# Mixture-of-experts stage of a decoder block: experts of at most 64 tokens computed with whole fp32 products from unsplit weights, in two halves of the output partitions

## The chip, the cores and the metric

The kernel runs on one core of one Trainium2 chip. The metric is the device time of one execution in microseconds (us). Three timed runs of the kernel before gave 1683.66, 1673.73 and 1675.67 us, so the median is 1675.67 us. One further execution was profiled; every row below comes from it.

## What is computed

The program is one decoder block over 512 tokens of width 1024: a Mamba-2 mixer and a pooling mixer, then a mixture of 64 experts of width 256 with one shared expert. Only the expert part matters here. The reference, cut to it:

```python
scores = jax.nn.sigmoid((uf @ w_router).astype(jnp.float32))
...
_, top_e = lax.top_k(masked, TOP_K)              # TOP_K = 8 of 64 experts for each of the 512 tokens
wts = wts / jnp.sum(wts, axis=-1, keepdims=True) * ROUTED_SCALE
...
def expert_block(args):                          # at most 128 tokens of one expert
    toks, ws, e = args
    xb = u_pad[toks]
    hid = jax.nn.silu(xb @ we_gate[e]) * (xb @ we_up[e])
    return (hid @ we_down[e]) * ws[:, None]
```

Everything is fp32. 512 tokens with 8 experts each make 4096 pairs. The reference's routing, evaluated on its own inputs, gives these sizes: 2 experts without a token, 32 with 1 to 64 tokens (the first expert, with 49, among them), 19 with 65 to 128, and 11 with more than 128 (at most 165).

## The kernel before

A product of two fp32 matrices is made of three products of reduced-precision halves (type fp32r). A tensor is split into a high part (a cast on ScalarE, line 44) and a low part (a subtraction on VectorE, line 45), and `mm3` (lines 58 to 62) adds high by high, high by low and low by high.

The function `experts` walks over the 64 experts in an order written out by hand (`manual_schedule`). An expert's weights arrive in three raw tiles of 1 MB, loaded by SyncE (`load`, lines 919, 920 and 926): two for gate and up, which together hold eight slices of the contraction, and one for down. There are eight raw tiles in turn, and `load(e + 2)` stands at the end of expert e. Each raw tile is split into a pair of fp32r tiles before use, which frees the raw tile. Expert e's body has, in order: the gate and up product (`gate_up_mm`, 8 slices of three matmuls of 512 columns), the splits of the next expert's first gate-and-up tile and of its own down tile, SiLU and multiply (`gate_act`, lines 946 and 947), the turning of the next expert's gathered tokens by eight TensorE transposes (`turn`, lines 883 to 889), the split of the next expert's second tile, the down product of the expert before (`down`, 12 matmuls), and the turning of the hidden activations (`down_in`, lines 956 to 958). After the body come the index of expert e + 4 (`slot_rows`, line 860), the scatter-add of the expert before (line 983, GpSimd) and the loads.

The number of an expert's tokens is known only at run time. So every engine holds all variants of a body and branches on a register: `n_e <= P` (line 1113), `n_e > 0` (line 1114). A variant for one block of tokens, one for none, and one for two blocks stand behind one another in each engine's program. The branches are instructions of the engine's sequencer, which runs ahead of the engine. The program is fetched from memory as the engine works through it; the profile shows these transfers as DMA queues of the kind "instruction".

Of the kernel before, what the change touches and what calls it, by code (L numbers as in the profile page):

```python
# [24 lines left out]
D = 1024  # L25
NK = 8
H = 32
G = 8
E = 64
NC = 8  # L30
# [814 lines left out]

def slot_onehot(k, pm, nb, eng):

    oh = k.wp.tile([P, NT, nb, P], BF16, name="oh", bufs=2)
    for t in range(NT):
        eng.tensor_scalar(oh[:, t], k.iota[:, :nb, :], pm[:, t:t + 1], None, op0=ALU.is_equal)  # L850
    return oh
# [24 lines left out]
def turn(k, src, x, full=None):  # L876

    nc = k.nc
    xv = src.rearrange("p (q k) -> p k q", k=NK)
    for hf in range(2):  # L880
        ps = k.xt.tile([P, 512], F32, name="xt", tag="xt")
        for q in range(4):
            nc.tensor.transpose(ps[:, q * P:(q + 1) * P], xv[:, hf * 4 + q, :], k.ident)  # L883
        ks = slice(hf * 4, hf * 4 + 4)
        pv = ps.rearrange("p (q t) -> p q t", q=4)
        if full is not None:
            nc.scalar.copy(full[:, ks, :], pv)
        nc.scalar.copy(x[0][:, ks, :], pv)  # L888
        nc.vector.tensor_sub(x[1][:, ks, :], pv, x[0][:, ks, :].bitcast(F32))  # L889
    return x  # L890


def split_pair(hp, lp):
# [48 lines left out]

def gate_act(k, ps):
# [70 lines left out]
def experts(k, shared):  # L1014
# [71 lines left out]
    gu[0][0].split(k, k.gu0w[0])  # L1086
    gu[0][1].split(k, k.gu1w)
    shared()
    onehot(4)
    load(1)  # L1090
    dn[0].split(k, k.dnw[0])
    turn(k, xg[0], k.xT[0])
    with tc.manual_schedule():
        fetch_over(0)
        fetch_over(1)
        for e in range(E):
            more = e + 1 < E
            xT, xnext = k.xT[e % 2], k.xT[(e + 1) % 2]
            hx, hlast = k.hx[e % 2], k.hx[(e + 1) % 2]
            fetch(e + 2)  # L1100

            def last_down(n):
                if e > 0:
                    down(k, hlast, dn[e - 1], n, k.yl[(e + 1) % 2], idx[e - 1][1][:, 0:1])

            def splits():
                if more:
                    gu[e + 1][0].split(k, k.gu0w[(e + 1) % 2])
                if e > 0:
                    dn[e].split(k, k.dnw[e % 2])  # L1110

            n_e = count(e, (ET.PE, ET.Activation, ET.DVE))
            with tc.If(n_e <= P) as big:
                with tc.If(n_e > 0) as some:
                    g0 = gate_up_mm(k, xT, gu[e])
                    splits()
                    hid = gate_act(k, g0)
                    if more:
                        turn(k, xg[e + 1], xnext)
                        gu[e + 1][1].split(k, k.gu1w)  # L1120
                    last_down(0)
                    last_down(1)
                    down_in(k, hid, hx)
                with some.Else():
                    splits()
                    if more:
                        turn(k, xg[e + 1], xnext)
                        gu[e + 1][1].split(k, k.gu1w)
                    last_down(0)
                    last_down(1)  # L1130
            with big.Else():
                turn(k, k.xg[3 + e % 2], xnext)
                g0 = gate_up_mm(k, xT, gu[e])
                splits()
# [4 lines left out]
                if more:  # L1139
                    turn(k, xg[e + 1], xnext)  # L1140
                last_down(0)
                down_in(k, hid1, k.hx[2])
                last_down(1)
                if more:
                    gu[e + 1][1].split(k, k.gu1w)
                for n in range(2):
                    down(k, k.hx[2], dn[e], n, k.xg[2], idx[e][1][:, 1:2])
            fetch_over(e + 2)
            onehot(e + 5)
# [6 lines left out]
        for n in range(2):  # L1156
            down(k, k.hx[e % 2], dn[e], n, k.yl[e % 2], idx[e][1][:, 0:1])
# [80 lines left out]
def block_kernel(ctx, tc, a, out):  # L1238
# [54 lines left out]
    with ExitStack() as p2:  # L1293
        raw2 = p2.enter_context(tc.tile_pool(name="raw2", bufs=2))
        k.wp = p2.enter_context(tc.tile_pool(name="wp", bufs=1))
        k.raws += [raw2.tile([P, 2048], F32, name="raw", tag="raw") for _ in range(2)]
        k.yl = [k.zp.tile([P, D], F32, name="yl", tag="zs") for _ in range(2)]
        k.hx = [tuple(k.wp.tile([P, 2, P], F32R, name=f"h{n}{i}") for n in "hl") for i in range(3)]
        spx = ExitStack()
        sp = spx.enter_context(tc.tile_pool(name="sp", bufs=1))  # L1300
# [45 lines left out]
```

## Time and profile before

| | |
|---|---|
| timed runs | 1673.73, 1675.67, 1683.66 us |
| profiled execution, whole | 1690.4 us |
| its span, first to last instruction | 1688.7 us |
| mean granted TensorE clock | 0.959 of full speed |
| bytes moved by DMA | 340.26 MB, mean 201 GB/s |

The page gives for each engine its busy time and its number of instructions. PE is TensorE's matmuls, PEld its weight loads, DVE is VectorE, ACT is ScalarE, POOL is GpSimd. An engine name with a "q" behind it is that engine's sequencer. In a timeline, the bracket at the end of a row is the idle time of the engine ahead of it and what ended it; "issue" there means that nothing the profile shows was waited for. A granted clock of 1.00 is 2.4 GHz and 0.50 is 1.2 GHz.

### The profile page before, as it was taken

The page shows a single profiled execution, that of the slowest core. Times are in us where ns is not written, and L with a number is a line of the kernel's source. Part 1 is how long each engine was busy: PE and PEld are TensorE (multiplying, and loading weights), DVE is VectorE, ACT ScalarE, POOL GpSimd, SP SyncE. Part 2 cuts the span into 40 slices and gives each one's busy share as a digit, 9 for nine tenths or more (in the row PEclk, how much of TensorE's full clock was granted, in tenths as well). Part 3 has the DMA queues.
Part 4 walks back from the last instruction along what each step waited for, and adds up shares of the span by engine and source line. Part 5 has one row for each costly group of instructions (what it writes and reads, how often), then busy time and mean ns, then how long its engine had stood idle before and what let it go on. Part 6 is the DMA issues. An engine that isn't in the chain of part 4 may idle for free.

```text
span 1688.7 us, 23424 instructions
## 1 busy us (share of the span) xinstructions
PE 1527.1 (90%) x7900; PEld 1267.4 (75%) x7900; DVE 1280.2 (76%) x1938; ACT 919.2 (54%) x1122; POOL 440.5 (26%) x312
## 2 busy tenths in 40 slices
PE   5999999999999999999898988898899988989980
PEld 5888788787888778887687776787677876777760
DVE  6888878778787974558666769776669889985856
ACT  3555545345343223335565657676567777775752
POOL 5211101002010110320233334332324233441426
PEclk7999999999999999999899999999999999999995
DMA  9442433333342345235967759868879988996954
GB/s 289 116 125 84 142 100 111 101 97 109 95 131 88 107 134 197 88 130 208 356 186 273 245 158 347 308 216 254 278 240 312 350 287 292 314 313 232 326 168 153
DMA packets 152118, 340.26 MB, mean 201 GB/s; under 512 B 15816, under 2 KB 94832, under 8 KB 142272
## 3 DMA queue, kind: packets, MB, share of 16 engines
q1 hardware_dynamic: 135888, 294.94, 51.8%
q0 software_dynamic: 15408, 40.23, 9.3%
q8 instruction: 120, 1.97, 0.5%
q10 hardware_dynamic: 576, 2.10, 0.3%
q14 instruction: 126, 1.03, 0.2%
HBM read 314.00 MB, written 31.01 MB: 204 GB/s over the span
## 4 chain that ended last, share of the span: by engine, by line
PE 53%; DMA 21%; issue 10%; DVE 9%; POOL 3%; ACT 3%; POOLq 0%; another core or an unknown queue 0%; SPq 0%; DVEq 0%; ACTq 0%
PE mm L62 8%; PE mm L60 8%; PE mm L61 8%; DMA xg<-u2d,idx 8%; DMA raw<-in_we_up_dram 5%; PE gu L60 4%; PE gu L62 4%; PE gu L61 4%; DMA Y<-xg,idx 4%; DVE wl L45 2%; DMA Y<-yl,idx 2%; PE xt L883 2%; PE sd L476 1%; PE yo L60 1%; PE yo L62 1%
## 5 line engine op out<-in xcount | busy, mean ns | idle before, releaser
L45 DVE TENSOR_TENSOR wl<-raw,wh 128x2048 fp32r<-128x2048 f32 x180 | 422.0, 2358 | 96.8 <-ACT wh L44 86.2
L44 ACT CAST wh<-raw 128x2048 fp32r<-128x2048 f32 x180 | 341.2, 1918 | 88.2 <-PE mm L61 64.2
L983 POOL DMA_INDIRECT Y<-yl,idx x64 | 132.5, 2070 | 482.6 <-ACT hh L957 238.5
L60 PE MATMUL gu<-wh,xh 128*128 128x512 f32 x444 | 184.0, 414 | 8.6 <-issue 6.6
L62 PE MATMUL gu<-wh,xl 128*128 128x512 f32 x444 | 180.3, 406 | 2.1 <-issue 2.1
L61 PE MATMUL gu<-wl,xh 128*128 128x512 f32 x444 | 180.5, 407 | 0.4 <-DVE hl L958 0.4
L60 PE MATMUL mm<-uh,wh 128*128 128x512 f32 x432 | 171.2, 396 | 1.9 <-ACT zs L284 1.9
L62 PE MATMUL mm<-uh,wl 128*128 128x512 f32 x432 | 169.8, 393 | 0.0
L61 PE MATMUL mm<-ul,wh 128*128 128x512 f32 x432 | 169.0, 391 | 0.0
L45 DVE TENSOR_TENSOR pair<-raw,pair 128x2048 fp32r<-128x2048 f32 x66 | 148.5, 2289 | 25.2 <-ACT pair L44 18.4
L871 POOL DMA_INDIRECT xg<-u2d,idx x75 | 126.0, 1680 | 97.6 <-DVE oh L850 27.5
L946 ACT ACTIVATE hid<-gu 128x256 f32<-128x256 f32 x73 | 28.1, 385 | 203.6 <-PE gu L62 203.6
L44 ACT CAST pair<-raw 128x2048 fp32r<-128x2048 f32 x66 | 123.2, 1923 | 15.8 <-DMA raw<-in_ws_up_dram 12.4
L883 PE MATMUL xt<-ident,xg 128*128 128x128 f32 x632 | 89.8, 286 | 36.7 <-issue 20.3
L883 PEld LDWEIGHTS xt<-ident,xg 128*128 128x128 f32 x632 | 84.0, 194 | 43.6 <-issue 36.2
L889 DVE TENSOR_TENSOR xl<-xt,xh 128x512 fp32r<-128x512 f32 x150 | 96.9, 685 | 20.3 <-ACT xh L888 18.8
L60 PEld LDWEIGHTS gu<-wh,xh 128*128 128x128 f32 x444 | 87.9, 198 | 27.5 <-issue 8.1
L888 ACT CAST xh<-xt 128x512 fp32r<-128x512 f32 x150 | 81.5, 590 | 45.2 <-PE xt L883 42.1
L61 PEld LDWEIGHTS gu<-wl,xh 128*128 128x128 f32 x444 | 87.6, 197 | 23.6 <-issue 3.9
L62 PEld LDWEIGHTS gu<-wh,xl 128*128 128x128 f32 x444 | 87.2, 196 | 20.5
L60 PEld LDWEIGHTS mm<-uh,wh 128*128 128x128 f32 x432 | 81.2, 188 | 20.2 <-ACT zs L284 2.3
L947 DVE TENSOR_TENSOR hid<-hid,gu 128x256 f32<-128x256 f32 x73 | 30.4, 417 | 85.7 <-ACT hid L946 85.7
(341 smaller groups left out, 3568.7 us busy)
## 6 DMA issues: line engine op xcount, KB each, us to landing
raw<-in_we_gate_dram SPq DMA_DIRECT2D x124, 512.0 KB
raw<-in_we_up_dram SPq DMA_DIRECT2D x124, 512.0 KB
raw<-in_we_down_dram SPq DMA_DIRECT2D x62, 1024.0 KB
raw<-in_w_in_dram SPq DMA_DIRECT2D x27, 1024.0 KB
raw<-in_w_ada_dram SPq DMA_DIRECT2D x16, 1024.0 KB
big<-in_w_ada_dram SPq DMA_DIRECT2D x16, 512.0 KB
raw<-in_w_in_dram SPq DMA_DIRECT2D x16, 512.0 KB
raw<-in_w_br_ssd_dram SPq DMA_DIRECT2D x8, 1024.0 KB
```

The lines of the kernel that those rows point to most:

```text
L44: nc.scalar.copy(h, raw)
L45: nc.vector.tensor_sub(l, raw, h.bitcast(F32))
L60: nc.tensor.matmul(out, sh, mh, start=first, stop=False)
L61: nc.tensor.matmul(out, sh, ml, start=False, stop=False)
L62: nc.tensor.matmul(out, sl, mh, start=False, stop=last)
L871: k.nc.gpsimd.indirect_dma_start(out=xg[:n], out_offset=None, in_=k.u2d, bounds_check=T - 1, oob_is_err=False, in_offset=bass.IndirectOffs ...
L883: nc.tensor.transpose(ps[:, q * P:(q + 1) * P], xv[:, hf * 4 + q, :], k.ident)
L888: nc.scalar.copy(x[0][:, ks, :], pv)
L889: nc.vector.tensor_sub(x[1][:, ks, :], pv, x[0][:, ks, :].bitcast(F32))
L946: nc.scalar.activation(hid, ps[:, :256], AF.Silu)
L947: nc.vector.tensor_mul(hid, hid, ps[:, 256:])
L983: k.nc.gpsimd.indirect_dma_start(out=k.Y[acc], out_offset=bass.IndirectOffsetOnAxis(ap=idx[0][:n, b:b + 1], axis=0), in_=y[:n], in_offset= ...
```

## The change

An expert with at most 64 tokens takes a variant of its own ("light"). Its weights are not split. `turn_light` turns 64 tokens in one PSUM tile and one copy, without a low part. `gate_up_light` multiplies in plain fp32 straight from the raw tiles: the tokens are the stationary operand (64 columns), gate fills partitions 0 to 63 of the output and up partitions 64 to 127, 16 matmuls of 256 columns. `act_light` turns both and applies SiLU and the product on the turned side. `down_light` does the same with the two halves of the 1024 output columns, 4 matmuls of 512 columns. Experts above 64 tokens are computed as before; the first expert always is. The branch for "no token" is gone: such an expert takes the light variant on what the tiles hold, its loads left out as before.

Because the variant of expert e needs the tokens of e + 1 turned, and the down product of e - 1 done, either of which may be light or not, each variant holds both forms of both steps behind branches of their own. The one-hot of the index moves from the body's end (for e + 5) to its start (for e + 4), in one buffer in place of two.

```diff
-    oh = k.wp.tile([P, NT, nb, P], BF16, name="oh", bufs=2)
+    oh = k.wp.tile([P, NT, nb, P], BF16, name="oh")
...
+def turn_light(k, src, x):
+
+    nc = k.nc
+    xv = src.rearrange("p (q k) -> p k q", k=NK)
+    ps = k.xt.tile([P, 512], F32, name="xt", tag="xt")
+    for kk in range(NK):
+        nc.tensor.transpose(ps[:, kk * LIGHT:(kk + 1) * LIGHT], xv[:LIGHT, kk, :], k.ident[:LIGHT, :LIGHT])
+    nc.scalar.copy(x, ps.rearrange("p (k t) -> p k t", k=NK))
...
+def gate_up_light(k, x, units):
+
+    nc = k.nc
+    ps = k.gu.tile([P, 512], F32, name="gu", tag="gu")
+    for kk in range(NK):
+        w = units[kk // 4].raw.rearrange("p (s k f) -> p s k f", k=4, s=2)
+        for s in range(2):
+            nc.tensor.matmul(ps[s * LIGHT:(s + 1) * LIGHT, :256], x[:, kk, :], w[:, s, kk % 4, :], start=kk == 0, stop=kk == NK - 1)
+    return ps
+
+
+def evict_light(k, ps):
+    hid = k.wp.tile([P, 256], F32, name="hid", bufs=2)
+    k.nc.scalar.copy(hid, ps[:, :256])
+    return hid
+
+
+def act_light(k, hid, x):
+
+    nc = k.nc
+    hv = hid.rearrange("p (q j) -> p j q", j=2)
+    ps = k.ht.tile([P, 2, P], F32, name="ht", tag="ht")
+    for j in range(2):
+        nc.tensor.transpose(ps[:, j, :], hv[:, j, :], k.ident)
+    nc.scalar.activation(x, ps[:, :, :LIGHT], AF.Silu)
+    nc.vector.tensor_mul(x, x, ps[:, :, LIGHT:])
+
+
+def down_light(k, x, unit, y, w):
+
+    nc = k.nc
+    ps = k.yo.tile([P, 512], F32, name="yo", tag="yo")
+    for j in range(2):
+        for n in range(2):
+            nc.tensor.matmul(ps[n * LIGHT:(n + 1) * LIGHT, :], x[:, j, :], unit.raw[:, j * D + n * 512:j * D + n * 512 + 512],
+                             start=j == 0, stop=j == 1)
+    for n in range(2):
+        nc.scalar.activation(y[:LIGHT, n * 512:(n + 1) * 512], ps[n * LIGHT:(n + 1) * LIGHT, :], AF.Copy, scale=w[:LIGHT])
...
+    def by_count(e, engines, light, heavy):
+
+        if e == 0:
+            heavy()
+        elif e < E:
+            with tc.If(count(e, engines) <= LIGHT) as small:
+                light()
+            with small.Else():
+                heavy()
...
+            def light():
+                g = gate_up_light(k, k.xf, gu[e])
+                early_split(e + 1)
+                hid = evict_light(k, g)
+                turned(e + 1)
+                downs(e - 1)
+                act_light(k, hid, k.hT)
+
+            def one():
+                g = gate_up_mm(k, xT, gu[e])
+                early_split(e + 1)
+                split_down(e)
+                hid = gate_act(k, g)
+                turned(e + 1)
+                downs(e - 1)
+                down_in(k, hid, hx)
...
+            def heavy():
+                with tc.If(count(e, every) <= P) as single:
+                    one()
+                with single.Else():
+                    two()
+
+            by_count(e, every, light, heavy)
```

`early_split`, `turned`, `downs` and `split_down` wrap the steps named above; `early_split`, `turned` and `downs` each branch on the count of the expert that they serve. `two` is the body for two blocks, with the same wrapped steps in it.

TensorE's program before, at the place where the variant for one block ends and the variant for an empty expert begins (`ht` is the turned hidden tile, `xt` the turned tokens, `yo` the down product):

```order
L62 MATMUL yo<-pair,hl_6171 128x512
L956 MATMUL ht<-ident,hid 128x128 x2
L1114 UNCONDITIONAL_BRANCH
L883 MATMUL xt<-ident,xg_5332 128x128 x8
L60 MATMUL yo<-pair,hh_6170 128x512
```

From the branch to the start of the next expert stand the variant for none and the variant for two blocks, which an expert of one block jumps over.

TensorE's program now, the start of one expert (`gu<-raw,xf` is the light gate and up product, `yo<-raw,hT` the light down product; lines from 883 on stand one or more further down than before):

```order
L1150 COMPARE_AND_BRANCH
L1164 UNCONDITIONAL_BRANCH
L961 MATMUL gu<-raw,xf 64x256 x16
L1150 COMPARE_AND_BRANCH
L900 MATMUL xt<-ident,xg_5332 128x64 x8
L1150 UNCONDITIONAL_BRANCH
L884 MATMUL xt<-ident,xg_5332 128x128 x8
L1150 UNCONDITIONAL_BRANCH
L1150 COMPARE_AND_BRANCH
L988 MATMUL yo<-raw,hT 64x512 x4
L1150 UNCONDITIONAL_BRANCH
L61 MATMUL yo<-pair,hh_6172 128x512
```

The light variant now stands first, with both forms of the two wrapped steps in it; the variants for one block and for two blocks follow, each with both forms as well. A light expert jumps from its end over all of these; a heavy one jumps over the light variant first.

ScalarE's program before, one expert of one block (`wh` and `pair` are high parts of weights):

```order
L1113 COMPARE_AND_BRANCH
L1114 COMPARE_AND_BRANCH
L44 CAST wh<-raw 128x2048 x2
L946 ACTIVATE hid<-gu 128x256
L888 CAST xh_6486<-xt 128x512 x2
L44 CAST wh<-raw 128x2048
L979 ACTIVATE yl<-yo,wt 128x512 x2
L957 CAST hh_6172<-ht 128x256
L1114 UNCONDITIONAL_BRANCH
```

ScalarE's program now, the start of a light expert:

```order
L1150 COMPARE_AND_BRANCH
L1164 COMPARE_AND_BRANCH
L45 CAST wh<-raw 128x2048
L1164 UNCONDITIONAL_BRANCH x2
L967 COPY hid<-gu 128x256
L1150 COMPARE_AND_BRANCH
L901 COPY xf<-xt 128x512
L1150 UNCONDITIONAL_BRANCH
L889 CAST xh_6488<-xt 128x512 x2
L45 CAST wh<-raw 128x2048
L1150 UNCONDITIONAL_BRANCH
```

The casts of the next expert's weights now stand behind a branch on that expert's count, and its own down tile is not cast at all.

## Rows read from the trace of the kernel before

**Rows 1.** Busy us (instructions) by stretch: expert stage, single blocks.

```profile
core 0: us, PE busy (x) PEld busy (x) DVE busy (x) ACT busy (x) POOL busy (x), PEclk, DMA share, GB/s
797.00:1645.00 848.00, 762.68 (x3944) 628.46 (x3942) 646.03 (x935) 565.70 (x643) 287.61 (x150) 0.95 0.82 272
1278.00:1303.00 25.00, 24.50 (x141) 20.36 (x141) 24.61 (x34) 20.96 (x25) 8.40 (x4) 1.00 1.03 329
```

**Rows 2.** The page's DMA issues: down weights, and results of second blocks.

```profile
raw<-in_we_down_dram SPq DMA_DIRECT2D x62, 1024.0 KB
...
Y<-xg,idx POOLq DMA_INDIRECT x11, 6.3
```

**Rows 3.** Line 946, the SiLU of every block: ns min/median/max, first, last start.

```profile
L946 ACT ACTIVATE hid<-gu x73: 372/385/389, 814.6 to 1636.3; 128x256 f32<-128x256 f32 x73
```

**Rows 4.** ScalarE's timeline (start us, us), SiLU alone: three single blocks.

```profile
1298.57 0.39 ACT L946 ACTIVATE hid<-gu 128x256 f32<-128x256 f32 x1 [1.34 <-PE gu L62]
...
1313.00 0.38 ACT L946 ACTIVATE hid<-gu 128x256 f32<-128x256 f32 x1 [6.07 <-PE gu L62]
...
1322.69 0.39 ACT L946 ACTIVATE hid<-gu 128x256 f32<-128x256 f32 x1 [1.33 <-PE gu L62]
```

**Rows 5.** The same: an expert of two blocks, and the next expert.

```profile
1111.81 0.39 ACT L946 ACTIVATE hid<-gu 128x256 f32<-128x256 f32 x1 [1.30 <-PE gu L62]
...
1130.11 0.39 ACT L946 ACTIVATE hid<-gu 128x256 f32<-128x256 f32 x1 [1.36 <-PE gu L62]
```

**Rows 6.** TensorE's timeline at 1304 us, inside the gap of rows 4.

```profile
1303.93 0.40 PE L60 MATMUL gu<-pair,xh 128*128 128x512 f32 x1
1304.17 0.39 PE L61 MATMUL gu<-pair,xh 128*128 128x512 f32 x1
1307.60 0.79 PE L62 MATMUL gu<-pair,xl 128*128 128x512 f32 x1 [3.04 <-issue]
1308.19 0.63 PE L60 MATMUL gu<-pair,xh 128*128 128x512 f32 x1
```

**Rows 7.** What TensorE waited for, 797 to 1650 us: total, times, longest.

```profile
PE xt L883 <- issue: 20.3, 4, 6.0
PE gu L60 <- issue: 10.5, 4, 3.7
...
PE gu L62 <- issue: 8.3, 3, 3.2
PE ixp L860 <- issue: 7.8, 6, 3.1
...
PE gu L61 <- issue: 4.1, 2, 3.6
```

**Rows 8.** Branches on the count, by sequencer: times, ns shortest/median/longest.

```profile
L1113 PEldq COMPARE_BRANCH  x64: 64/75/5589, 808.0 to 1628.2; - x64
L1113 ACTq COMPARE_BRANCH  x64: 34/34/50, 810.8 to 1630.9; - x64
...
L1114 PEldq COMPARE_BRANCH  x106: 67/188/6792, 808.1 to 1637.2; - x106
```

**Rows 9.** The page's DMA queues, one of program code: packets, MB, share.

```profile
q8 instruction: 120, 1.97, 0.5%
```

**Rows 10.** The same queue in the expert stage, 797 to 1650 us.

```profile
q8 instruction: 89, 1.46, 0.7%
```

**Rows 11.** The same queue, 1416 to 1434 us, the weight queue full.

```profile
q8 instruction: 4, 0.07, 1.5%
```

**Rows 12.** The same queue, 1487 to 1491.5 us, the weight queue running empty.

```profile
q8 instruction: 2, 0.03, 2.7%
```

**Rows 13.** Groups: a weight tile's split, and a plain fp32 product.

```profile
L45 DVE TENSOR_TENSOR wl<-raw,wh 128x2048 fp32r<-128x2048 f32 x180 | 422.0, 2358 | 96.8 <-ACT wh L44 86.2
L44 ACT CAST wh<-raw 128x2048 fp32r<-128x2048 f32 x180 | 341.2, 1918 | 88.2 <-PE mm L61 64.2
...
L458 PE MATMUL sd<-xdec,Bt 128*128 128x256 f32 x48 | 14.7, 388 | 0.0
```

More of the change, by code (lines that the diff above doesn't have):

```diff
@@ L27 @@
 H = 32
+LIGHT = 64
 G = 8
@@ L1092, in experts, with early_split, late_split, turned @@
     turn(k, xg[0], k.xT[0])
+    every, both = (ET.PE, ET.Activation, ET.DVE), (ET.Activation, ET.DVE)
+    def by_count(e, engines, light, heavy):
[6 more added lines that the diff above has]
+                heavy()
+    def early_split(e):
+        if e < E:
+            for engines in (every, both):
+                count(e, engines)
+        def heavy():
+            gu[e][0].split(k, k.gu0w[e % 2])
+        if e < E:
+            with tc.If(count(e, both) > LIGHT):
+                heavy()
+    def late_split(e):
+        gu[e][1].split(k, k.gu1w)
+    def turned(e, split_too=True):
+        def heavy():
+            turn(k, xg[e], k.xT[e % 2])
+            if split_too:
+                late_split(e)
+        by_count(e, every, lambda: turn_light(k, xg[e], k.xf), heavy)
+    def downs(e, parts=(0, 1)):
+        if e < 0:
+            return
+        y, w = k.yl[e % 2], idx[e][1][:, 0:1]
+        def light():
+            if 0 in parts:
+                down_light(k, k.hT, dn[e], y, w)
+        def heavy():
+            for n in parts:
+                down(k, k.hx[e % 2], dn[e], n, y, w)
+        by_count(e, every, light, heavy)
+    def split_down(e):
+        if e > 0:
+            dn[e].split(k, k.dnw[e % 2])
     with tc.manual_schedule():
@@ L1096, in experts, with light, two @@
         for e in range(E):
-            more = e + 1 < E
             xT, xnext = k.xT[e % 2], k.xT[(e + 1) % 2]
-            hx, hlast = k.hx[e % 2], k.hx[(e + 1) % 2]
+            hx = k.hx[e % 2]
             fetch(e + 2)
[L1102 to L1131, printed above, removed]
+            onehot(e + 4)
+            for i in (e, e + 1):
+                if i < E:
+                    for engines in (every, both):
+                        count(i, engines)
+            def light():
+                g = gate_up_light(k, k.xf, gu[e])
[12 more added lines that the diff above has]
+                down_in(k, hid, hx)
+            def two():
                 turn(k, k.xg[3 + e % 2], xnext)
                 g0 = gate_up_mm(k, xT, gu[e])
-                splits()
+                early_split(e + 1)
+                split_down(e)
                 hid = gate_act(k, g0)
@@ L1138, in experts, with heavy @@
                 down_in(k, hid, hx)
-                if more:
-                    turn(k, xg[e + 1], xnext)
-                last_down(0)
+                turned(e + 1)
+                downs(e - 1)
                 down_in(k, hid1, k.hx[2])
-                last_down(1)
-                if more:
-                    gu[e + 1][1].split(k, k.gu1w)
                 for n in range(2):
                     down(k, k.hx[2], dn[e], n, k.xg[2], idx[e][1][:, 1:2])
+            def heavy():
+                with tc.If(count(e, every) <= P) as single:
+                    one()
+                with single.Else():
+                    two()
+            by_count(e, every, light, heavy)
             fetch_over(e + 2)
-            onehot(e + 5)
             if e > 0:
@@ L1155, in experts @@
         e = E - 1
-        for n in range(2):
-            down(k, k.hx[e % 2], dn[e], n, k.yl[e % 2], idx[e][1][:, 0:1])
+        downs(e)
         first(e, lambda n: scatter(k, idx[e], 0, k.yl[e % 2], 1, n))
@@ L1297, in block_kernel @@
         k.yl = [k.zp.tile([P, D], F32, name="yl", tag="zs") for _ in range(2)]
+        k.xf = k.wp.tile([P, NK, LIGHT], F32, name="xf")
+        k.hT = k.wp.tile([P, 2, LIGHT], F32, name="hT")
         k.hx = [tuple(k.wp.tile([P, 2, P], F32R, name=f"h{n}{i}") for n in "hl") for i in range(3)]
```

1 line of the change is left out of this document (removed).

## The prediction

> **What bounds the kernel now.** I read the stretches first, to see which engine fills the expert stage. Over its 848 us TensorE is busy for 763, VectorE for 646, and the DMA engines for a share of 0.82 [rows 1]. Where single blocks follow each other undisturbed, TensorE is busy for 24.5 of 25 us and VectorE for 24.6: two engines at their limit, with DMA full at 329 GB/s [rows 1]. An expert's weights are 3.1 MB, so at 329 GB/s they take 9.6 us.
>
> Next, the cadence. From the first to the last SiLU of the stage there are 821.7 us [rows 3], that is 63 steps from expert to expert. An undisturbed step of a single block takes 9.7 us (1313.00 to 1322.69) [rows 4]; an expert of two blocks takes 18.3 us [rows 5]. The reference's routing says which steps there are after the first expert: 31 light with tokens, 2 without, 19 of 65 to 128, 11 above 128. The trace agrees where it can: down weights for 62 experts, second blocks for 11 [rows 2]. So the steps cost 50 x 9.7 + 11 x 18.3 = 686 us, the two empty ones some 6 us each (splits, turning and a down product without gate and up), together 698. The other 124 us are disturbance.
>
> What disturbs it is the point on which I build. One step took 14.4 us in place of 9.7 [rows 4]. In it TensorE stopped for 3.04 us between two matmuls of one accumulation, with "issue" as the reason, so no data and no engine was waited for; the matmul just behind took 0.63 us instead of 0.39 [rows 6]. Such idle time sums to 51 us in 19 waits [rows 7]. Most of the remainder is matmuls at the lower clock behind these stops: the mean granted clock is 0.95 [rows 1]; with only the levels 0.5 and 1, a tenth of 848 us ran at half rate, which costs about 42.
>
> The branches tell where the stops come from. On TensorE's sequencer a branch on the count normally takes 75 or 188 ns, but up to 5.6 and 6.8 us; on ScalarE, whose program has 2,337 rows in the order listing against TensorE's 13,205, never over 50 ns [rows 8]. The profile has a queue that carries program code: 120 packets, 1.97 MB [rows 9]. Counting the order listing of the kernel before (a matmul and its weight load as two, a plain fp32 product as two such pairs, because 24 of them stand as 48 records [rows 13]) gives 30,000 instructions for TensorE. Over 120 packets that is 250 each, so this queue is TensorE's and it fetches the whole program, the variants that are jumped over too. The stage takes 89 of the packets [rows 10], 1.39 per expert. A stop is a packet that is late.
>
> The Trainium skill, page "Runtime: NRT & Kernel Launch", section "Instruction fetch mechanics", says that code comes in 16 KiB blocks, one after the other, and that a taken branch out of the blocks at hand waits for the target to be fetched. By that rule, the trace agrees: 1.97 MB over 120 packets is 16.4 kB, and a branch waited 6.8 us [rows 8, 9].
>
> **What the change does, part by part.**
>
> Splits removed: 33 light experts (all but the first) lose three casts of 1.92 us on ScalarE and three subtractions of 2.36 us on VectorE [rows 13], 190 and 234 us of busy time. Alone this is worth nothing, because TensorE's 9.7 us per step stand beside it; it only takes away the second limit.
>
> Products changed: gate and up are 16 plain products of 256 columns, two records each. Such a record lasts 388 ns [rows 13], like an fp32r matmul of 512 columns, and those start 0.24 us apart [rows 6]. So 32 x 0.24 = 7.7 us, and the down product 8 records of twice the columns, 3.8 us. Turning and index: 9.7 less 36 x 0.24, 1.1 us. One after the other, a light step is 12.6 us of TensorE against 9.7 now. If the two halves of the output partitions run at once, it is 11.5 / 2 + 1.1 = 6.9 us. No row of before shows two products side by side, so both ends stay in the range. I take the lower, since the next term covers both within 0.3 us.
>
> The Trainium skill, page "TensorEngine Tiling (Array Packing)", section "Theoretical Speedup", gives up to twofold speed for at most 64 stationary columns. By it a light step would be near 6.9 us on TensorE; no run here shows it yet.
>
> Code added: this is the term that decides. Counted from the order listing in the same way, one expert's section of TensorE's program had 342 instructions (one block 92, none 40, two blocks 184, index and branches 26). It now has about 522 (light 140, one block 124, two blocks 216, index and branches 42), because both forms of the turning and of the down product stand in each variant. The whole program grows from 30,000 to 41,600. So an expert needs 1.39 x 522 / 342 = 2.12 packets. How fast do they come? With the weight queue full, four in 18 us although TensorE waited for them [rows 11], 4.5 to 6 us each, and single waits reached 5.6 and 6.8 [rows 8]; with the weight queue running empty, two within 4.5 us [rows 12]. I take 5.8 us. That makes 12.3 us per expert, above the 9.7 of a single block, the 6.9 to 12.6 of a light one, and the 9.6 of its weights.
>
> Jumps added: a light expert jumps over about 340 instructions, more than one packet; a heavy one jumps over 140 ahead of its own variant, an expert of two blocks over 140 and 124. Now only experts of two blocks jump at their start, and the longest "issue" waits, four of 20.3 us in all, are at the transposes, with which such an expert opens [rows 7]. I give each of the 11 experts of two blocks 7 us for this; for the others it is inside the 12.3.
>
> Moved: the one-hot goes ahead of the body, so the index waits less; 0. Raw tiles are held until the product has read them, the down tile one expert longer. With eight tiles and three per expert, and 9.6 us of loading against 12.3 of code, the loads have cover; without it they would be late by at most a tile, 3.2 us per step. Shorter branches on ScalarE and VectorE cost about 50 ns each [rows 8]; 0.
>
> Sum for the 63 steps: light and empty 33 x 12.3 = 406; single blocks 19 x 12.3 = 234; two blocks 11 x (18.3 + 7) = 278; together 918 us against 821.7, so +96. From the profiled execution's 1690.4 us this makes 1786. That execution is 15 us above the median of the runs shown, 1675.67, so I forecast 1772 us.
>
> **The rivals.**
>
> Code does not bind (faster). If the longer jumps skip packets, or packets come ahead when an expert needs little else, light steps fall to the loads' 9.6 us, single blocks stay at 9.7, two blocks at 18.3, and half of the 124 us of disturbance stays: 317 + 184 + 201 + 62 = 764, that is -58: 1618 us. For it: there are only 19 stops in 63 steps now [rows 7], and half of the branches take 188 ns or less [rows 8]. Against: now no packet is skipped [rows 9], and waits of 5 us and more exist at 1.39 packets per step already. It decides below 4.9 us per packet, where 52 x 2.12 x 4.9 + 278 gives the stage's present length.
>
> The Trainium skill, page "Runtime: NRT & Kernel Launch", section "Instruction fetch mechanics", calls the crossing from one block to the next mostly hidden. By that sentence the code term would vanish and this rival would hold.
>
> Halves run one after another, and code waits come in series with them. Then a light step is 12.6 us plus one stop of 3 us [rows 6], 15.6 in place of 12.3: 33 x 3.3 = +109, 1881 us. For it: no row shows halves at once.
>
> The clock falls. TensorE waits in every step, and behind a stop of 3 us a matmul took 0.63 in place of 0.39 us [rows 6]. With light work at half rate a step is 2 x 6.9 = 13.8 us: 33 x 1.5 = +50, 1822 us.
>
> **How the numbers follow.** Forecast 0.60, no binding code 0.15, halves in series 0.14, clock 0.11. The forecast's own spread comes from the packet time: at 5.0 us a light or single step is 10.6 us and the stage 829, 1683 us in all; at 6.8 us it is 14.4 and the stage 1028, 1882 us. I cut the range where 0.1 is left on each side: 1685 to 1855 us. A measurement tells about 1% from no change, 17 us. Faster by more: the first rival, and little of the forecast, 0.16. Within 1%: 0.07. Slower: the rest, 0.77.
>
> **What would show it.** Right: the code queue carries about 165 packets in place of 120; light steps lie 11 to 13 us apart; "issue" is TensorE's largest wait in the stage, several times 51 us; ScalarE and VectorE have much idle time. Wrong: steps of light experts at 9.6 us or below with DMA full, or fewer than 130 code packets, would mean that code does not bind. If TensorE is busy without gaps through light steps, the products bind, not the code.

## The result and the profile after

The changed kernel takes 1813.66 us (median of 4, 1809.11 to 1817.89) against 1678.67 (1673.73 to 1683.66) for the kernel before on the same chip: a ratio of 1.0804, 95% interval 1.0757 to 1.0851. It is slower by 135 us, beyond the forecast of 1772 us and inside its range.

Busy times of the expert stage, from the first to the last hidden activation of its experts (engine columns as in [rows 1]); the first row is the kernel before, the second the changed kernel:

```profile
core 0: us, PE busy (x) PEld busy (x) DVE busy (x) ACT busy (x) POOL busy (x), PEclk, DMA share, GB/s
814.60:1636.30 821.70, 740.33 (x3821) 611.84 (x3821) 634.36 (x897) 553.63 (x627) 281.57 (x144) 0.95 0.83 275
816.90:1762.00 945.10, 720.42 (x4010) 537.82 (x4011) 363.56 (x703) 371.25 (x499) 220.47 (x144) 0.87 0.72 240
```

The stage lasts 945.1 us where it lasted 821.7 [rows 3], so it is 123 us longer and holds nearly the whole loss. Over it VectorE is busy for 364 us and ScalarE for 371, against 634 and 554 over those 821.7 us before. The work that the change was to save is gone. TensorE, too, is busy for 20 us less than before (740), the DMA engines move 240 GB/s in place of 275, and the granted clock is 0.87 in place of 0.95. No engine and no transfer is nearer its limit than it was.

The page's code queue, which answers to [rows 9], and the branches on the count, which answer to [rows 8] (ns shortest, median, longest; first and last start):

```profile
q8 instruction: 165, 2.70, 0.6%
...
L1150 PEldq COMPARE_BRANCH  x288: 64/187/6969, 812.7 to 1763.3; - x144
L1150 ACTq COMPARE_BRANCH  x288: 34/38/55, 816.9 to 1764.5; - x144
...
L1243 PEldq COMPARE_BRANCH  x51: 69/218/5567, 810.4 to 1762.9; - x51
```

165 packets in place of 120. The same branch takes ScalarE 55 ns at most and TensorE up to 6.97 us. In the stage TensorE's branches of over 1 us were 10 and summed to 41.6 us; now they are 59 and sum to 281.9 us (added up from the trace's branch rows).

That these branches wait for code can be read from the trace too: 58 of the 59 hold the landing of a packet of the code queue and end 1.3 to 1.6 us after it. And they account for the loss. TensorE is without a matmul for 225 us of the stage in place of 81; of this, 154 us lie inside a long branch in place of 29. That is 125 us more, for a stage that is 123 us longer.

What TensorE waited for from 790 to 1780 us (us in total, times, longest), in answer to [rows 7]:

```profile
PE ixp L861 <- issue: 55.4, 19, 6.2
PE xt L884 <- issue: 52.4, 11, 7.0
PE ixp L861 <- DVE hT L979: 24.5, 10, 5.5
PE yo L61 <- ACT hh L1008: 15.9, 12, 1.9
PE gu L61 <- issue: 15.9, 4, 6.5
PE gu L61 <- ACT wh L45: 12.7, 3, 6.6
```

All rows with "issue" come to 134 us in 43 waits (the three shown to 124 in 34), against 51 in 19 before. The other rows partly hide the same cause, as the next piece shows. It is TensorE's weight-load side in the timeline (start us, us, then the idle time before it), in the step from a light expert (50) to one of 96 tokens (51):

```profile
1578.83 0.31 PEld L977 LDWEIGHTS ht<-ident,hid 128*128 128x128 f32 x2 [0.81 <-issue]
1582.23 0.26 PEld L861 LDWEIGHTS <-oh 128*128 128x128 bf16 x8 [3.09 <-issue]
1588.47 0.29 PEld L61 LDWEIGHTS gu<-pair,xh 128*128 128x128 f32 x1 [5.97 <-issue]
```

TensorE leaves the light body and stands for 3.09 us; it computes the index and stands for 5.97 us before its first product. The trace has one branch at 1576.41 us that takes 5.77 us and the next at 1582.26 that takes 5.79 (the first begins while earlier matmuls still run). Packets of the code queue start at 1579.63 and 1585.52 us, inside these two branches, and take 1.0 us each. The branches are the jumps over the two other bodies of expert 50 and over the light body of expert 51. On TensorE's own row the second wait is put down to a cast on ScalarE; the branch alone spans it.

The steps between first activations, by the kind of the expert left and entered, show where the 123 us lie (light: up to 64 tokens; single: 65 to 128, and the first expert, which is always computed whole; double: over 128):

| step | number | before, us in all | after, us in all |
|---|---|---|---|
| single to light | 8 | 78 | 63 |
| light to light | 16 | 176 | 209 |
| light to single or double | 13 | 177 | 264 |
| out of a double one | 11 | 203 | 211 |
| through the two empty experts (before, they have no activation) | 4 | 44 | 55 |
| single to single or double | 11 | 144 | 143 |

The 13 steps from a light expert to a heavier one lose 87 of the 123 us, the light-to-light steps 33. The long branches lie there too: 24 of the 59, with 130 us, in those 13 steps, 17 with 86 us in the light-to-light ones, and 3 with 7 us in the steps from single to light.

### The profile page after: what moved, and what is told of

Read it like the earlier page. It is cut to its first block, busy times and chain, and to the rows that moved or that the text cites. A ratio compares the mean times of both kernels' runs of the same rounds, so it can differ in the third digit from the quotient of the medians.

```text
span 1813.5 us, 24669 instructions
## 1 busy us (share of the span) xinstructions
PE 1507.5 (83%) x8084; PEld 1192.6 (66%) x8084; DVE 1008.4 (56%) x1744; ACT 736.6 (41%) x994; POOL 379.4 (21%) x312
## 5 line engine op out<-in xcount | busy, mean ns | idle before, releaser
L46 DVE TENSOR_TENSOR wl<-raw,wh 128x2048 fp32r<-128x2048 f32 x114 | 273.0, 2400 | 109.8 <-ACT wh L45 95.1
L45 ACT CAST wh<-raw 128x2048 fp32r<-128x2048 f32 x114 | 216.5, 1906 | 135.4 <-PE mm L62 65.8
L961 PE MATMUL gu<-raw,xf 128*64 128x256 f32 x1056 | 145.6, 431 | 13.0 <-issue 6.4
L961 PEld LDWEIGHTS gu<-raw,xf 128*64 128x64 f32 x1056 | 105.5, 156 | 39.6 <-issue 19.0
L61 PE MATMUL gu<-wh,xh 128*128 128x512 f32 x256 | 109.1, 426 | 19.8 <-ACT pair L45 6.9
L62 PE MATMUL gu<-wl,xh 128*128 128x512 f32 x256 | 106.8, 417 | 1.1 <-issue 1.1
L63 PE MATMUL gu<-wh,xl 128*128 128x512 f32 x256 | 106.1, 415 | 0.8 <-issue 0.8
L46 DVE TENSOR_TENSOR pair<-raw,pair 128x2048 fp32r<-128x2048 f32 x33 | 75.0, 2291 | 54.9 <-ACT pair L45 44.0
L63 PEld LDWEIGHTS mm<-uh,wl 128*128 128x128 f32 x432 | 81.6, 189 | 17.6 <-issue 0.9
L62 PEld LDWEIGHTS mm<-ul,wh 128*128 128x128 f32 x432 | 81.5, 189 | 17.0 <-issue 0.4
```

The costliest lines, as they stand in the source:

```text
L45: nc.scalar.copy(h, raw)
L46: nc.vector.tensor_sub(l, raw, h.bitcast(F32))
L61: nc.tensor.matmul(out, sh, mh, start=first, stop=False)
L62: nc.tensor.matmul(out, sh, ml, start=False, stop=False)
L63: nc.tensor.matmul(out, sl, mh, start=False, stop=last)
L961: nc.tensor.matmul(ps[s * LIGHT:(s + 1) * LIGHT, :256], x[:, kk, :], w[:, s, kk % 4, :], start=kk == 0, stop=kk == NK - 1)
```

## The experiments

All are built from the two kernels; each was timed beside the kernel before on one chip.

**Light code present, not used** (NONE is 0).

```diff
-            with tc.If(count(e, engines) <= LIGHT) as small:
+            with tc.If(count(e, engines) <= NONE) as small:
...
-            with tc.If(count(e, both) > LIGHT):
+            with tc.If(count(e, both) > NONE):
```

> The changed kernel with the test for the light form set to a count of 0 in place of 64: only the two empty experts take it, all others compute with the split weights as the kernel before does. The program is as long as that of the changed kernel (41,581 instructions of TensorE). Theory C (TensorE's program code binds: more packets per expert and longer jumps): 165 code packets, TensorE's branches above 1 us sum to 200 us or more in the stage, and the time is 1780 to 1870 us although the light products are gone. Rival L (the light products themselves, their halves or the chain around them, cost the time): 1670 to 1700 us. Rival H (raw tiles are held longer by the light products, so loads come late): also 1670 to 1700 us, with the DMA share back at 0.8.

1821.26 us, ratio 1.0886 (1.0843 to 1.0929), DMA share 0.72, and 54 branches of over 1 us that sum to 196 us. The queue and the test's row:

```profile
q8 instruction: 165, 2.70, 0.6%
...
L1151 PEldq COMPARE_BRANCH  x195: 64/218/6617, 812.2 to 1768.7; - x195
```

With the arithmetic of the kernel before the loss is still there, so neither the light products nor the tiles that they hold cause it. The tests inside the step are still in this program, so it doesn't tell them from the code; the next run does.

**The kernel before with code that never runs.** The three bodies stay inside the first branch; the second holds the body for two blocks once more.

```diff
+            with tc.If(n_e <= 400) as real:
...
+            with real.Else():
...
```

> The kernel before with one more copy of the two-block body per expert, in a branch that no expert takes (a count above 400): 41,866 instructions of TensorE in place of 30,002, the same arithmetic. Theory C by throughput (every packet is fetched, 5.8 us each, 2.14 per expert, so 12.4 us for a step without a second block): 165 packets and 1760 to 1860 us. Theory C by jumps (a packet costs time only where a branch leaves what is already fetched; here one more jump over 184 instructions per expert): 165 packets, and 1690 to 1760 us. Rivals L and H (nothing of the code matters): 1670 to 1690 us.

1825.59 us, ratio 1.0901 (1.0868 to 1.0934). The packets, and the test between one block and two, which stood in line 1113:

```profile
q8 instruction: 168, 2.75, 0.6%
...
L1115 PEldq COMPARE_BRANCH  x106: 67/310/6865, 811.7 to 1770.4; - x106
```

This is the change's loss without a line of the change: 53 branches of over 1 us, 222 us in all, and each of the 53 holds the landing of a code packet. One test per expert came with the copy, around the whole body; there is none inside a step. The number fits the reading by throughput, not the one by single jumps.

**The form chosen when the program is built: heavy, light, and light with the halves in series.** The first is the kernel before, the others the changed one, with the tests replaced by the counts of this input:

```diff
-            with tc.If(count(e, engines) <= LIGHT) as small:
-                light()
-            with small.Else():
-                heavy()
+            light() if CNT[e] <= LIGHT else heavy()
```

> The kernel before with the form of each expert chosen when the program is built, from the counts of this input, so that TensorE, ScalarE and VectorE have one form per expert and no branch (16,326 instructions of TensorE, 65 packets). The choice at run time by count is left out on these three engines. Theory C: the 124 us of disturbance go for the most part, steps of 9.7 and 18.3 us remain: 1560 to 1610 us. Rivals L and H: the time of the kernel before, 1670 to 1690 us, since the arithmetic and the loads are the same.

> The changed kernel with the form of each expert chosen when the program is built, from the counts of this input (16,694 instructions of TensorE); the choice at run time is left out on TensorE, ScalarE and VectorE. This is what the light products are worth without the code. Theory C: light steps fall to the 8 to 9.6 us of products and loads, 1530 to 1590 us, that is 0 to 55 us below the same without light products. Rivals L and H: the loss stays, 80 to 140 us above the same without light products.

1591.35 us heavy, ratio 0.9492 (0.9459 to 0.9525), and 1590.14 us light, ratio 0.9497 (0.9467 to 0.9527). The stage's row of the heavy form, with 63 packets:

```profile
822.00:1538.70 716.70, 705.80 (x3821) 589.95 (x3820) 626.01 (x896) 551.72 (x627) 300.25 (x144) 0.99 0.92 313
```

and of the light form, with 65:

```profile
818.40:1530.10 711.70, 660.41 (x4010) 479.93 (x4010) 356.99 (x702) 367.78 (x498) 237.30 (x144) 0.97 0.92 315
```

Code and tests together had cost the kernel before some 85 us. The tests by themselves took little of it, since an undisturbed step lasts 9.7 us with them [rows 4] and without. Without code and tests the light form relieves VectorE by 269 us and TensorE by 45, and the time is the same to 1 us: both forms draw weights at a share of 0.92, 313 and 315 GB/s. Light-to-light steps are mostly 6.9 to 8.0 us against 9.7, but some take 13 to 18, and steps from a light to a double expert 12.1 against 10.6: what is gained in one step is given back in another. In the longest of these light steps, of 18.3 us, TensorE waits for weights in the midst of a product, with the DMA engines at a share of 1.03:

```profile
1280.61 3.03 PE L963 MATMUL gu<-raw,xf 128*64 128x256 f32 x14 [2.53 <-DMA raw<-in_we_up_dram]
```

How much of the light form's time the weights set was not tested by itself; it has no run without the loads. So the change had nothing to win here even with free code. The gain of 0 to 55 us that I expected came out at its lower end.

The loops over j and n of the down product are exchanged in the same way:

```diff
-    for kk in range(NK):
-        w = ...
-        for s in range(2):
+    for s in range(2):
+        for kk in range(NK):
+            w = ...
             nc.tensor.matmul(ps[s * LIGHT:(s + 1) * LIGHT, :256], x[:, kk, :], w[:, s, kk % 4, :], ...)
```

> The kernel with light products and the form chosen when the program is built, with the two loops of each light product exchanged: all matmuls of the one half of the output partitions first, then those of the other, so that neighbours in the program write the same partitions. The same instructions in another order. If neighbours on different halves run at once, gate and up take 7.4 us in place of 3.7 and down 3.8 in place of 1.9: a light step grows from about 8 to about 13.5 us, by 33 x 3.9 (above the 9.6 us of the loads) = 100 to 180 us in all. If the halves don't run at once, or overlap in any order: the same time within 1%.

1632.98 us (2 runs), 43 us more than with the halves alternating; less than the 100 I gave as the lower end. TensorE's timeline of one light gate and up product, alternating:

```profile
1419.27 3.67 PE L963 MATMUL gu<-raw,xf 128*64 128x256 f32 x32
```

and one half after the other:

```profile
1470.98 6.31 PE L963 MATMUL gu<-raw,xf 128*64 128x256 f32 x32
```

The halves do run at once if neighbours in the program lie on different halves. The down product kept its 1.94 us in either order: its records still start in pairs, though four of one half came first. So only 2.64 us per light expert were added, 87 for 33, and half of that did not show in the time.

**Without the weight loads.**

```diff
         elif e < E:
             gu[e], dn[e] = [Unit(k), Unit(k)], Unit(k)
-            with tc.If(count(e, (ET.SP,)) > 0):
-                load_gu(k, a.we_gate[0, e], a.we_up[0, e], gu[e])
-                load_down(k, a.we_down[0, e], dn[e])
```

> The changed kernel without the weight loads of the experts from the fifth on: they compute with weights that lie in the tiles from earlier experts. All else, the program of TensorE too, is the same. It asks whether the 5.8 us of a code packet are its own or come from sharing the DMA engines with the weights. If from sharing: TensorE's long branches shrink from about 5.8 us to 2 to 4 us, packets come 3 to 4 us apart where they are waited for, and the time falls to 1540 to 1650 us. If a packet has its 5.8 us by itself: long branches as before, over 200 us in all, and 1760 to 1815 us.

1655.05 us (2 runs), ratio 0.9846 (0.9766 to 0.9926), 5 us above the range that I gave. The stage takes 785.6 us, and the branches of over 1 us are 54 with 177 us, 3.3 us each, where the changed kernel has 4.8 each:

```profile
816.40:1602.00 785.60, 685.28 (x4009) 505.75 (x4010) 363.92 (x703) 370.47 (x499) 235.03 (x144) 0.94 0.26 56
...
L1147 PEldq COMPARE_BRANCH  x288: 64/187/5746, 812.7 to 1603.2; - x144
```

Light-to-light steps fall from 13.0 to 9.1 us, steps from light to single from 18.8 to 13.3. The program is as long (163 packets), so a packet is dear partly because of the weight traffic. The average of 4.8 us also depends on the way through the program: with the light code not used it is 3.6 us with the weights flowing. Cleaner are the long branches that start within 1 us of the end of another one, so that there was hardly time to fetch ahead. The changed kernel has 11 of them, of 5.9 us in the median: 3.5 us until the packet starts, 1.1 for the packet, and 1.4 until the branch ends. Without the loads there are 10, of 3.2 us: 0.7, 1.2 and 1.4. So the weight traffic lengthens the wait ahead of a packet and not its transfer; code isn't free without it. How much of the 159 us came through shorter stops, and how much because TensorE no longer waited for weights, this run doesn't separate.

**Each form once per expert.** The changed kernel's nested bodies are written one behind the other.

```diff
+            by_count(e, every, lambda: gate_up_light(k, k.xf, gu[e], g), lambda: gate_up_mm(k, xT, gu[e], g))
+            early_split(e + 1)
...
+            by_count(e, both, lambda: evict_light(k, g, hid), heavy_act)
+            with tc.If(count(e, every) > P):
+                turn(k, k.xg[3 + e % 2], xnext)
+                gate_act(k, gate_up_mm(k, xnext, gu[e]), hid1)
+            turned(e + 1)
+            downs(e - 1)
+            by_count(e, every, lambda: act_light(k, hid, k.hT), lambda: down_in(k, hid, hx))
+            with tc.If(count(e, every) > P):
...
```

> The changed kernel with its branches written one behind the other, a test for each step (gate and up, turning, down, activation, and two for second blocks), so that each form of a step stands once per expert: 28,880 instructions of TensorE in place of 41,581, with the light products as in the changed kernel, and more but shorter jumps. The index, the loads and the queues stay. Theory C by throughput: 115 packets, 1.35 per expert or 7.8 us, so that loads (9.6 us) and products (10 to 11 us for a single block) bind again: 33 x 9.6 + 19 x 10.5 + 11 x 19 = 725 us and some 60 of disturbance in the stage, 1600 to 1680 us, below the kernel before. Theory C by jumps: branches still wait, some two long ones per expert of 65 tokens and more, 1690 to 1780 us. Rivals L and H: within 2% of 1814 us, since the light products and the raw tiles are unchanged.

1775.74 us, ratio 1.0601 (1.0565 to 1.0637). 114 packets, one fewer than forecast, and the long branches are gone but for 6 with 13 us. But a new wait has come, for VectorE's sequencer to reach the test for a second block:

```profile
PE xt L884 <- DVEq L1220: 95.0, 26, 10.4
PE ht L1006 <- DVE hl L1008: 22.8, 11, 3.0
```

The time lies in the range given for jumps, but not for its reason. I next took these two waits away (against the kernel just above):

```diff
+            with tc.If(count(e, every) > P):
+                turn(k, k.xg[3 + e % 2], xnext)
             by_count(e, every, lambda: gate_up_light(k, k.xf, gu[e], g), ...)
...
+            by_count(e, every, lambda: act_light(k, hid, k.hT[e % 2]), lambda: down_in(k, hid, hx))
             downs(e - 1)
-            by_count(e, every, lambda: act_light(k, hid, k.hT), lambda: down_in(k, hid, hx))
```

> The kernel with one branch per step once more, with three moves: the turning of a second block stands ahead of the gate and up product in a test of its own, the activation stands ahead of the down product of the expert before, and the tile hT is doubled for it. 29,072 instructions of TensorE. In the run with one branch per step TensorE waited 95.0 us in 26 waits at its transposes for VectorE's sequencer to reach the test for a second block, and 22.8 us in 11 for the second block's transposes. Theory C by throughput (fewer packets are what counts; what was left there was this new wait): both waits go, 1776 less 70 to 118, so 1655 to 1710 us, with TensorE's long branches still under 20 us. Theory C by jumps (six tests per expert cost what the code saves): 1740 to 1790 us.

1710.38 us, ratio 1.0217 (1.0184 to 1.0251), 65 us less, at the upper end of the range for throughput. What is left at TensorE ends at sequencers again:

```profile
PE ht L975 <- DVEq L1149: 24.5, 9, 5.5
PE ht L1006 <- DVEq L1222: 15.4, 8, 3.3
PE xt L884 <- PEq L1222: 12.0, 21, 0.6
PE gu L960 <- ACTq L1210: 11.4, 17, 0.8
```

**The same idea on the kernel before: one body, three tests.**

```diff
+            with tc.If(n_e > P):
+                turn(k, k.xg[3 + e % 2], xnext)
             g0 = gate_up_mm(k, xT, gu[e])
...
+            with tc.If(n_e > P):
+                gate_act(k, gate_up_mm(k, xnext, gu[e]), hid1)
...
+            with tc.If(n_e > P):
...
```

> The kernel before, without light products, with one body per expert for one block, two blocks and none: the gate and up product, the turning, the down product of the expert before and the activation stand once and without a test, and three tests on the count (above 128) add what a second block needs. 21,890 instructions of TensorE in place of 30,002. An empty expert computes its product from the weights that lie in the tile, and nothing of it is scattered. Theory C by throughput: 87 packets, 1.0 per expert in the stage or 5.8 us, under the 9.7 us of a step; of the 85 us that the form fixed at build time gained over the kernel before, most comes: 1600 to 1640 us. Theory C by jumps (a packet costs where a branch leaves what is fetched): three short jumps per expert stay, 1640 to 1690 us. If neither the number of packets nor the jumps matter: within 1% of the kernel before.

1739.62 us, ratio 1.0351 (1.0286 to 1.0416): outside every range that I gave. 86 packets, and no long branch at all:

```profile
L1120 PEldq COMPARE_BRANCH  x75: 73/208/352, 811.4 to 1677.4; - x75
```

Yet each of the 16 light-to-light steps takes 11.2 to 11.8 us (11.44 on average), where the undisturbed step of before is 9.7. So few packets alone don't make a fast program. In such a step TensorE's gaps end where a sequencer reaches one of the three tests:

```profile
1313.60 1.13 PE L883 MATMUL xt<-ident,xg 128*128 128x128 f32 x8 [0.30 <-PEq L1120]
1315.04 0.51 PE L957 MATMUL ht<-ident,hid 128*128 128x128 f32 x2 [0.31 <-DVEq L1120]
...
1319.15 0.48 PE L60 MATMUL gu<-pair,xh 128*128 128x512 f32 x1 [0.35 <-ACTq L1128]
```

This body also does the activation ahead of the down product, the other way round than before. The next run has one test, at the start of the step, splits the down weights ahead of it, and has the old order again:

```diff
+            if e > 0:
+                dn[e].split(k, k.dnw[e % 2])
+            with tc.If(n_e > P):
...
+            g0 = gate_up_mm(k, xT, gu[e])
...
```

> The kernel before with one body per expert and one test for all of a second block, at the start of the step; the down weights are split ahead of it. 21,506 instructions of TensorE, as many packets as in the run with a shared body and three tests (86), where no branch waited long and yet a step of one block took 11.5 us in place of 9.7. Theory D (a test inside a step costs about 0.6 us at TensorE, because the engines meet there, and three of them gave the 1.8 us): with one test a step is about 10.3 us; 1591 us of the form fixed at build time, plus 62 x 0.6 = 37, plus 11 x 3 for the bare starts of second blocks = 33, so 1640 to 1685 us. If the loss there came from the program in another way (its packets or the order of down product and activation): 1710 to 1745 us.

1717.20 us, ratio 1.0223 (1.0181 to 1.0265), above the 1640 to 1685 us of theory D and inside the 1710 to 1745 us that I had given for another cause. The time alone thus speaks against theory D; the single steps speak for it in part. Light to light takes 10.0 us on average, from 9.8 to 10.5, so the test and the earlier split cost 0.3 us together. The two further tests cost 0.7 us each ((11.44 - 10.0) / 2) if the changed order costs nothing; no run moved the order alone. Most of the miss lies at the second block, which now has nothing beside it:

```profile
PE gu L62 <- DVE xl L889: 23.1, 11, 2.8
PE gu L60 <- ACT xh L888: 23.0, 11, 2.4
PE ht L957 <- DVE xg L948: 10.8, 11, 1.0
```

That is 5.2 us per double expert, not 3, and a step from a light to a double one takes 17.0 to 19.6 us where the fixed form takes 10.6 (here its second block comes first). With 19 us for the tests and 57 for these waits the fixed form's 1591 us become 1667; the other 50 us lie at the double experts too and are not accounted for in full. A part is the clock: in the double expert at 898 to 938 us, the matmuls behind the waits take 0.63 us in place of 0.39, and the granted clock is 0.66 from 908 to 918 us.

**A shorter program without more tests: no body for empty experts.**

```diff
             with tc.If(n_e <= P) as big:
-                with tc.If(n_e > 0) as some:
-                    g0 = gate_up_mm(k, xT, gu[e])
...
-                with some.Else():
...
+                g0 = gate_up_mm(k, xT, gu[e])
...
```

> The kernel before without the body for an empty expert (and without its test): one body for up to 128 tokens, one above. The two empty experts compute from the weights that lie in the tiles, and nothing of it is scattered. 27,354 instructions of TensorE in place of 30,002, 302 per expert in place of 342, and no test inside a step. Theory C by throughput: 109 packets in place of 120. The change under study lost 123 us of stage with 45 packets more, 2.7 us each; 11 fewer give back 20 to 30 us: 1640 to 1665 us. If packets only cost time above some length of an expert that 342 has not reached: 1670 to 1690 us.

1635.13 us, ratio 0.9721 (0.9685 to 0.9758), against 1679.52 for the kernel before: faster than both kernels. 107 packets, and the long branches fall from 10 (41.6 us) to 3 (16.4 us):

```profile
q8 instruction: 107, 1.75, 0.4%
...
L1113 PEldq COMPARE_BRANCH  x117: 64/188/5967, 808.0 to 1588.0; - x117
```

It gave back 44 us, more than the 15 to 40 of the range: 13 fewer packets, of which each was worth 3.4 us. Some of it may be the second test that went with the body; the two were not separated, but an undisturbed step has 9.7 us in both kernels, so a test around a whole body costs it nothing that shows. All 16 light-to-light steps are now 9.4 to 10.0 us.

## Why the prediction held

**Code decides: shown.** The program's length was forecast exactly (165 packets), and the sign of the change was right. The kernel before slows by 9% when code that never runs is added to it, the changed kernel stays slow when its light products are not used, and both come to 1590 us when the forms are fixed. The long branches hold the landings of code packets, and TensorE's idle time inside them grew by 125 us. Where the bodies stay whole, one behind the other or nested, the time goes with the packets (number, then time): 63, 1591 us; 65, 1590; 107, 1635; 120, 1679; 165, 1814; 168, 1826. Tests inside a step are a rival that the prediction doesn't have. They have a price of their own, as the runs with 114 and 86 packets show; but the copy that never runs brings no such test and loses as much.

**The signs.** The packets came out as said, and ScalarE and VectorE are idle for most of the stage. The light-to-light steps average 13.0 us, but they spread from 8.3 to 17.5, not from 11 to 13. "Issue" grew to 134 us, 2.6 times 51 and not several times: part of the waiting stands in rows of other engines.

**Splits removed, worth nothing alone: shown** by the two fixed forms, 1591 and 1590 us.

**Light products.** I took 6.9 us of TensorE's time per light step. Gate and up take 3.67 (forecast 3.84), down 1.94 (1.92), turning 1.09, with transposes and index 0.84: 7.5 us. These spans overlap a little: in the fixed form, undisturbed steps between light experts that follow a third one take 6.9 to 7.3 us. So the 6.9 us held, and with them the assumption that the halves run at once.

**Code time per step, and jumps.** I forecast 12.3 us for every light and single step and 7 us more for each double expert, together +96 us; the stage grew by 123. The packet time was right: where one long branch followed another, a packet took 5.9 us in the median (forecast 5.8). How the stops fall on the steps was not. Added up as in the forecast's sum, by the expert that is left:

| term | forecast | measured |
|---|---|---|
| 33 light and empty | 33 x 12.3 = 406 us | 528 us, 16.0 each |
| 19 single | 19 x 12.3 = 234 us | 206 us, 10.9 each |
| 11 double | 11 x 25.3 = 278 us | 211 us, 19.1 each |

The errors of +122, -28 and -67 us leave 27, so that the total came this close is in part luck. The step that failed is "I give each of the 11 experts of two blocks 7 us for this; for the others it is inside the 12.3". The terms of the light experts came out too small by it, and those of the double experts too large. The price does not lie at double experts as such but above all at the steps from a light expert to a heavier one, where two jumps follow each other: over about 340 instructions, more than a packet of 250, and over 140. Those 13 steps take 20.3 us each on average (264 / 13). Single to light takes 7.9; there the light body comes first in the program and nothing is jumped over on the way in. That this order is the reason is a reading of the program; no run moved the bodies.

The Trainium skill, page "Runtime: NRT & Kernel Launch", section "Instruction fetch mechanics", says that a taken branch out of the fetched window waits. The trace agrees: 5.77 and 5.79 us. The same section calls block crossings mostly hidden; here that held for the fixed forms (63 and 65 packets, "issue" waits of at most 0.3 us), and not for the kernel before, where TensorE stopped for 3.04 us between two matmuls of one accumulation, without a branch [rows 6]; a code packet starts in that gap, at 1305.15 us.

**One-hot, raw tiles, shorter branches on ScalarE and VectorE at 0:** none of them shows. The run with the light code not used has the longer hold at the two empty experts alone and loses as much; ScalarE's longest branch is 55 ns. The one-hot wasn't moved alone, so its 0 is argued only.

**The rivals.** Code that does not bind fell at the first two runs. Halves in series: they run at once, and made to run in series they cost 43 us, not 109. The falling clock is real (0.87 in the stage) but follows the stops: in the fixed light form, with the same products, it is 0.97. In the forecast I gave clock and stops as separate cases; here they come together.

## What to carry to other kernels

Before a run-time variant is added to an unrolled kernel, count TensorE's instructions per unit of work: here each code packet beyond the kernel before cost about 3 us (135 us for 45 packets, and 153 for 48 of code that never runs). Shorten the program by dropping a rare body whose work is harmless to do anyway (44 us here), not by cutting a body into many tested pieces: with three tests inside it (and two parts in another order) a step grew by 1.7 us, and with six TensorE waited 95 us for another engine's sequencer. And ask first what the cheaper arithmetic is worth with free code: fixing the forms at build time, of the kernel before and of the changed one, answers that; here the answer was nothing.

## What was not expected of the hardware

- Matmuls of 64 stationary columns on the two halves of the output partitions run at once only if they are near each other in the program: 3.67 us alternating, 6.31 us with 16 records of one half first; with 4 records first (the down product) nothing was lost.
- A never-taken variant costs as much as a used one: 1826 us with dead code, 1814 with the light code.
- A code packet's wait depends on the weight traffic: a long branch right behind another took 5.9 us beside it and 3.2 without (medians), while the packet's own transfer took 1.1 and 1.2 us.
- A test that doesn't wait for code still costs TensorE time when it stands inside a step: 10.0 us with one and 11.2 to 11.8 with three (where the order of two steps changed too), against 9.7 with tests around the whole body or with none.
